# Relative bias written as eight rows and copied in DRAM for 128 queries, and RWKV's low-rank weights loaded and split in the indexer

## The chip, the cores and the metric

The kernel runs on one core of a Trainium2 chip. Times are device microseconds (us) of one execution. The kernel before took 1330.21 us, the median of 3 runs (1328.97 to 1335.14).

The engines are PE (TensorE: matrix products; PEld is its weight load), DVE (VectorE), ACT (ScalarE), POOL (GpSimd) and SP (SyncE, which issues nearly all DMAs of this kernel). Each engine takes its own instructions strictly in their order.

## What is computed

One inference step of a layer with three groups of heads, for 1024 new prompt rows and 64 new sample rows with 512 rows of history (1088 rows in all):

```
z = rms_norm(h, norm_g) @ w_in          # all branch columns from one projection
A: RWKV-7     zm = z + (prev - z) * mu;  r, k, v, w_in, a_in = split(zm)
              decay = exp(-exp(-softplus(-(w0 + tanh(w_in) @ w_b)) - 0.5))
              a     = sigmoid(a0 + a_in @ a_b)
              S = S * w + (S @ -kk) (kk * a)^T + v k^T;   y = S r   # a scan over the rows
B: forgetting attention
C: sparse attention: an indexer scores keys, the 256 best are kept,
              s = q . k * scale + t5_table[t5_bucket(pos_k - pos_q)]
h = h + concat(A, B, C gated) @ w_out;   y = rms_norm(h, final_g)
```

Two things matter here. `w_b` and `a_b` (64 x 512 each) are RWKV's low-rank weights. The relative bias of branch C depends on the distance of key and query alone: 8 heads by 384 distances hold all of it.

## The kernel before

The stages follow one another in one program: norm and transposes, the **indexer** (`indexer`), **RWKV** (17 units of four chunks, whose parts are braided), then the two attentions and the output. The projection `z` is made in column pieces of up to 128 (`proj`, L154: for each of 8 k-blocks three products, of `wb` with `uL` and of `wh` and `wl` with `uH`, for 384, 384 and 320 rows in turn). Its pieces are "fill": generators that `pump` calls between the steps of the main work. In the indexer the fill is the group `a0` of RWKV's columns and then `a1`.

A weight piece takes this way (`load_w`): SP issues the load of 512 KB into `wraw` (L130; two buffers), ACT casts it into `wh` (L137), POOL makes `wl` (L140, four instructions) and `wb` (L142, two). A product of the projection leaves PSUM from one of two banks, by ACT (`zs`, L802) and DVE (`zm`, L803, and `shift`, L805 and L806).

The order on each engine is not the order of the code alone. The framework's scheduler lays the instructions out by a simulated time line and by priorities, and takes what is ready in it; so a DMA that the code issues late can stand early in SP's queue.

**The bias.** `relative_bias` is a generator. Its first step loads the table and a one-hot matrix (L1250, L1251), its second makes the 8 x 384 product on PE (L1254) and copies it to `t5v` in SBUF, 8 partitions of 384 numbers (L1256). The third issues one DMA (L1258) that writes these eight rows 128 times into `d_t5` in DRAM, once for each of 128 queries. In the code the steps stand at i = 3, 5 and "s" of the indexer's loop over query blocks. `d_t5` is read again by the sparse attention (L1155). The profile calls it `d_t`.

**The low-rank weights.** `rwkv_pools`, behind the indexer, allocates `wabh` and `wabl`, clears `wabl` on POOL (L1271), loads each weight twice, for both halves of the partitions, into `wabr`, a buffer of the ring `z` (L1275, four DMAs of 128 KB), casts it on ACT (`wabh`, L1276) and makes the differences on POOL (`wabl`, L1278, two instructions). Each RWKV unit then begins with the products `low_rank` (L1293 with `wabh`, L1294 with `wabl`), with `wt` (L853), which is read back from DRAM, as the other operand, and with sums over squares (L1331).

Of the kernel before, what the change touches and what calls it, by code (L numbers as in the profile page):

```python
# [12 lines left out]
F32 = mybir.dt.float32  # L13
F32R = mybir.dt.float32r
# [4 lines left out]
OP = mybir.AluOpType  # L19
# [5 lines left out]
P = 128  # L25
# [60 lines left out]
class K:  # L86
# [311 lines left out]
    def indexer(self):  # L398
# [6 lines left out]
        with ExitStack() as c2:  # L405
# [54 lines left out]
            for i in list(range(2, 8)) + ["s"]:  # L460

                if i == 3:
                    gates = self.forget(ip, mrow)
                    next(gates)
                    bias = self.relative_bias(c2)
                    next(bias)
                if i == 4:
                    nc.sync.dma_start(out=O["p_c_kidx"][0, 0].rearrange("(a p) d -> p a d", p=P), in_=mrow[:, 0:8, 0:64])
                    nc.sync.dma_start(out=O["s_c_kidx"][0, 0], in_=mrow[:64, 8, 0:64])
                if i == 5:  # L470
                    next(bias)
                if i == 7:
                    next(gates, None)
                if i == "s":
                    next(bias, None)
                r = P if i != "s" else 64
                q0 = i * P - 256 if i != "s" else 768
                k0, kn = (0, (i + 1) * P) if i != "s" else (1024, 576)
                wi = 8 if i == "s" else i
                for s0 in range(0, kn, 512):  # L480
                    n = min(512, kn - s0)
                    for h in range(4):
                        ps = pm.tile([P, 512], F32, tag="s", name="ps_idx")
                        nc.tensor.matmul(ps[:r, :n], QI[h][:, q0:q0 + r], KI[:, k0 + s0:k0 + s0 + n], start=True, stop=False)
                        nc.tensor.matmul(ps[:r, :n], QI[h][:, q0:q0 + r], KIL[:, k0 + s0:k0 + s0 + n], start=False, stop=True)
                        rl = ip2.tile([P, 512], F32, tag="rl", name="rl")
                        nc.scalar.activation(rl[:r, :n], ps[:r, :n], AF.Relu, scale=0.125)
                        dst = self.score[i][:r, s0:s0 + n]
                        if h == 0:
                            nc.vector.tensor_scalar(dst, rl[:r, :n], wI[:r, wi, 0:1], None, op0=OP.mult)  # L490
                        else:
                            nc.vector.scalar_tensor_tensor(dst, rl[:r, :n], wI[:r, wi, h:h + 1], dst, op0=OP.mult, op1=OP.add)
                        if h % 2:
                            yield
                if i != "s":
                    nc.vector.memset(self.score[i][0:64, kn - 64:kn], NEG)
# [745 lines left out]
    def relative_bias(self, ctx):  # L1242

        nc = self.nc
        self.d_t5 = self.dram.tile([P, 8, 384], F32, tag="d_t5", name="d_t5")
        p = self.pool("t5", ctx=ctx, right=True)
        pp = self.pool("t5p", space=PSUM, ctx=ctx, right=True)
# [7 lines left out]
        vv = p.tile([8, 384], F32, name="t5v")  # L1255
        nc.vector.tensor_copy(vv, ps[:8, :384])  # L1256
        yield
        nc.sync.dma_start(out=self.d_t5.rearrange("q h r -> h q r"), in_=vv.rearrange("h (o r) -> h o r", o=1).broadcast_to([8, P, 384]))  # L1258


    def rwkv_pools(self, c2):


        nc, I, O = self.nc, self.I, self.O
        one = self.pool("rw1", ctx=c2, right=True)
        self.gen = self.pool("gen", space=PSUM, ctx=c2)
        self.gring = lambda tag, bufs: (lambda dt=F32: self.gen.tile([P, 512], dt, tag=tag, name="ps_" + tag, bufs=bufs))

        self.wabh = one.tile([P, 2, 512], F32R, name="wabh")
        self.wabl = one.tile([P, 2, 512], F32R, name="wabl")  # L1270
        nc.gpsimd.memset(self.wabl.bitcast(F32), 0.0)  # L1271
        raw = self.z("wabr")[:, 0:1024].rearrange("p (x c) -> p x c", x=2)
        for x, nm in enumerate(("a_w_b", "a_a_b")):
            for r in (slice(0, 64), slice(64, 128)):
                nc.sync.dma_start(out=raw[r, x], in_=I[nm][0])  # L1275
        nc.scalar.copy(self.wabh, raw)  # L1276
        for x, r in enumerate((slice(0, 64), slice(64, 128))):
            nc.gpsimd.tensor_tensor(self.wabl[r, x], raw[r, x], self.wabh[r, x], op=OP.subtract)  # L1278
        self.one, self.state = one, None

        self.ND = [one.tile([P, 2, 4, P], F16, name=f"ND{i}") for i in range(2)]
        for t in self.ND:
            nc.gpsimd.memset(t, 0.0)
# [472 lines left out]
def program(ctx, tc, I, O):  # L1756
# [24 lines left out]
    s.setup()  # L1781
    cx.close()
    with ExitStack() as c2:
        s.zs = s.pool("zs", bufs=1, ctx=c2, right=True)
        s.scp = s.pool("scp", ctx=c2, right=True)
        s.tkp = s.pool("tkp", ctx=c2, right=True)
# [19 lines left out]
        for u in range(n + 2):  # L1806
# [12 lines left out]
            if u < n:  # L1819
                work.append(("topk", topk, N_TOPK, (DVE, ACT)))  # L1820
            work = [w[:3] for w in work if w[0] != "topk"]
            s.free = u >= FE
            s.braid(work, R_T if u > n else R_END if len(work) < 3 and u else R_A / 10, ("topk", topk, N_TOPK, (DVE, ACT), work[-1][0] if SIDE < 0 else work[SIDE][0]) if u < n else None)
        for _ in topk:
# [89 lines left out]
```

## Time and profile before

| what | number |
|---|---|
| median of 3 runs | 1330.21 us |
| the profiled execution's own time | 1331.56 us |
| its span, first to last instruction | 1329.8 us |
| PE busy | 1258.4 us, 95% of the span |
| DVE, ACT, POOL busy | 847.5, 780.2, 669.7 us |
| mean granted clock of PE | 0.979 of full speed |
| DMA moved | 168.78 MB, mean 127 GB/s |

The numbers of the trace are from one profiled execution, whose span lies 1.8 us below its own time. "Busy" of PE is the time in which a product is under way, also at a lower clock. "Idle before" an instruction, in brackets in the time line, is the time in which its engine had nothing to do, with the work that ended the wait.

### The profile page before, as it was taken

The numbers are of one execution on the slowest core, as the hardware profiler recorded it, in microseconds if no ns is written. First come the engines' busy times: TensorE is split into PE (matmuls) and PEld (weight loads), VectorE is DVE, ScalarE is ACT, GpSimd is POOL, SyncE is SP. The second block draws the span as 40 slices with busy tenths as digits, with TensorE's granted clock in tenths as the row PEclk, the third lists the DMA queues.
The fourth block names the chain that finished last, engine by engine and source line by source line (L and its number), as shares of the span: only waits on it lengthen the run. The fifth ranks groups of instructions, "written<-read, shape, count | busy, mean of one in ns | idle before, by whom it ended". The sixth has DMA issues, their size and how long they took to land.

```text
span 1329.8 us, 29357 instructions
## 1 busy us (share of the span) xinstructions
PE 1258.4 (95%) x10544; PEld 964.2 (73%) x10563; DVE 847.5 (64%) x2487; ACT 780.2 (59%) x1762; POOL 669.7 (50%) x973
## 2 busy tenths in 40 slices
PE   7969999999999999988999998999999989999997
PEld 5747676777777777766777677888988856777764
DVE  7338437887877777899754316556666479766642
ACT  7335427777777887644353346576665578655532
POOL 6223445445445456556464365566667567544311
PEclk9979999999999999988999998999999989999999
DMA  7352422222223324433232378867755576543323
GB/s 224 50 105 71 128 83 66 87 70 89 68 70 104 102 80 140 123 101 110 94 104 89 126 216 246 217 201 209 182 198 146 146 212 186 142 116 106 97 76 95
DMA packets 172460, 168.78 MB, mean 127 GB/s; under 512 B 38513, under 2 KB 147097, under 8 KB 172314
## 3 DMA queue, kind: packets, MB, share of 16 engines
q1 hardware_dynamic: 172314, 166.89, 43.9%
q8 instruction: 84, 1.38, 0.4%
q14 instruction: 62, 0.51, 0.1%
HBM read 104.61 MB, written 62.24 MB: 125 GB/s over the span
## 4 chain that ended last, share of the span: by engine, by line
PE 73%; DVE 11%; DMA 6%; ACT 3%; issue 3%; POOL 2%; SPq 1%; DVEq 0%; POOLq 0%; ACTq 0%
PE pproj L154 32%; PE pproj L1697 7%; PE ps_pv L993 5%; PE ps_atp L107 5%; PE ps_tp L1697 4%; PE ps_ga L1412 3%; DMA wraw<-in_w_in_dram 2%; PE ps_sc L962 2%; PE ps_sc L963 2%; PE ps_gb L1471 2%; PE ps_tp L107 1%; PE ps_gb L1478 1%; PE ps_gc L1581 1%; ACT junka L601 1%; PE ps_gc L1583 1%
## 5 line engine op out<-in xcount | busy, mean ns | idle before, releaser
L154 PE MATMUL pproj<-uH,wh 128*128 128x384 f32 (+4 forms) x1088 | 494.6, 455 | 0.0
L154 PE MATMUL pproj<-uH,wl 128*128 128x384 f32 (+4 forms) x1088 | 363.4, 334 | 0.0
L154 PE MATMUL pproj<-uL,wb 128*128 128x384 bf16 (+4 forms) x1088 | 359.4, 330 | 2.2 <-DVE shift L806 2.0
L154 PEld LDWEIGHTS pproj<-uH,wh 128*128 128x128 f32 (+1 forms) x1088 | 217.9, 200 | 3.9 <-issue 0.7
L154 PEld LDWEIGHTS pproj<-uH,wl 128*128 128x128 f32 (+1 forms) x1088 | 208.1, 191 | 2.2 <-issue 0.2
L154 PEld LDWEIGHTS <-wb 128*128 128x128 bf16 (+1 forms) x1088 | 106.6, 98 | 118.6 <-issue 81.5
L601 ACT ACTIVATE junka<-score,tk_tau 128x1024 f16<-128x1024 f32 (+4 forms) x160 | 149.4, 934 | 38.9 <-DVE junk L595 24.1
L914 POOL TENSOR_SCALAR S<-S,mx 128x128 f32<-128x128 f32 (+8 forms) x136 | 103.8, 766 | 83.7 <-DVE mx L913 60.4
L931 ACT CAST hl<-ps_atp 128x512 fp32r<-128x512 f32 (+3 forms) x184 | 93.4, 514 | 77.7 <-PE ps_atp L107 68.2
L140 POOL TENSOR_TENSOR wl<-wraw,wh 128x256 fp32r<-128x256 f32 (+1 forms) x184 | 137.1, 775 | 3.3 <-ACT wh L137 2.7
L932 DVE TENSOR_TENSOR hl<-ps_atp,hl 128x512 fp32r<-128x512 f32 (+3 forms) x184 | 109.7, 600 | 44.6 <-ACT hl L931 42.8
L142 POOL TENSOR_SCALAR wb<-wraw 128x512 bf16<-128x512 f32 (+1 forms) x92 | 60.3, 671 | 142.1 <-issue 60.7
L909 ACT ACTIVATE S<-S,mx 128x128 f32<-128x128 f32 (+8 forms) x136 | 105.8, 778 | 38.2 <-DVE mx L905 34.8
L993 PE MATMUL ps_pv<-hl,VS 128*128 128x256 f32 (+3 forms) x640 | 113.7, 290 | 7.7 <-ACT hl L931 3.2
L993 PEld LDWEIGHTS ps_pv<-hl,VS 128*128 128x128 f32 (+1 forms) x640 | 90.4, 176 | 20.8 <-DVE hl L932 5.0
L107 PE MATMUL ps_atp<-ident,S 128*128 128x128 f32 x616 | 103.6, 280 | 1.1 <-POOL S L914 0.8
L1159 POOL TENSOR_TENSOR cb<-nm,T 128x256 f32<-128x256 bf16 (+2 forms) x80 | 57.4, 724 | 52.7 <-DVE mx L905 51.1
L107 PEld LDWEIGHTS ps_atp<-ident,S 128*128 128x128 f32 x616 | 76.4, 144 | 7.7 <-issue 1.7
L137 ACT CAST wh<-wraw 128x1024 fp32r<-128x1024 f32 (+1 forms) x46 | 47.7, 1038 | 47.0 <-PE pproj L154 27.0
L1697 PE MATMUL pproj<-oh,gh 128*128 128x512 f32 x144 | 67.4, 490 | 0.6 <-ACT pproj L1745 0.3
L803 DVE SCALAR_TENSOR_TENSOR zm<-pproj,omm,zs 128x384 f32<-128x384 f32 (+2 forms) x52 | 25.8, 496 | 43.3 <-ACT zs L802 42.9
L1697 PE MATMUL pproj<-ol,gb 128*128 128x512 bf16 (+1 forms) x134 | 48.8, 386 | 1.4 <-DVE ol L1677 0.9
(383 smaller groups left out, 2849.6 us busy)
## 6 DMA issues: line engine op xcount, KB each, us to landing
wraw<-in_w_in_dram SPq DMA_DIRECT2D x45, 512.0 KB
oraw<-in_w_out_dram SPq DMA_DIRECT2D x12, 512.0 KB
out_dram<-rows SPq DMA_DIRECT2D x10, 512.0 KB
x<-in_x_prompt_dram SPq DMA_DIRECT2D x8, 512.0 KB
wt<-a_wa SPq DMA_DIRECT2D x16, 256.0 KB
b_v<-vs SPq DMA_DIRECT2D x8, 512.0 KB
VS<-b_v SPq DMA_DIRECT2D x8, 512.0 KB
d_y<-y SPq DMA_DIRECT2D x64, 64.0 KB
```

Of the source, the lines that this page charges most:

```text
L107: self.nc.tensor.transpose(out, x, self.ident[:n, :n])
L140: nc.gpsimd.tensor_tensor(l[:, k:k + 2, :n], raw[:, k:k + 2, :n], h[:, k:k + 2, :n], op=OP.subtract)
L142: nc.gpsimd.tensor_scalar(b[:, k:k + 4, :n], raw[:, k:k + 4, :n], 1.0, 0.0, op0=OP.mult, op1=OP.add)
L154: self.nc.tensor.matmul(ps[:n, :nt], a[:, k, :n], b[:, k, t0:t0 + nt], start=(k == 0 and i == 0), stop=(k == KD - 1 and i == 2))
L601: nc.scalar.activation(junk[:, :sc.shape[1]], sc, AF.Sign, bias=tf[:, j:j + 1], accum_out=cnt[:, j:j + 1])
L909: nc.scalar.activation(S[:, :kn], S[:, :kn], AF.Exp, bias=mx[:, nm - 1:nm], scale=-1.0, accum_out=mx[:, 6:7])
L914: nc.gpsimd.tensor_scalar(S[:, :kn], S[:, :kn], mx[:, 7:8], 0.5, op0=OP.mult, op1=OP.mult)
L931: nc.scalar.copy(ph[:kr, a:b], ps[:kr, a:b])
L932: nc.vector.tensor_tensor(pl[:kr, a:b], ps[:kr, a:b], ph[:kr, a:b], op=OP.subtract)
L993: nc.tensor.matmul(pv[0:m, q0:256], VS[:, kb, 0:m], hl[:, x, o:o + w], start=kb == 0 and x == 0, stop=at[-1][0] == last and n == 3)
L1159: nc.gpsimd.tensor_tensor(o, x, y, op=OP.add)
L1697: nc.tensor.matmul(ps[hf][:n, :], parts[m // 4][q][:, m % 4, :n], self.wo[m][q // 2][:, hf * 512:hf * 512 + 512], start=m == 0 and q == 0, ...
```

## The change

It has two parts.

**The bias** is written as eight rows only: `t5v` goes to a new DRAM tile `d_row` (8 x 384), and eight DMAs copy `d_row` from DRAM to DRAM, each into 16 of the 128 queries of `d_t5`. In the code the row is written at i = "s" of the indexer's loop, and the copies are issued one by one at the beginning of RWKV's units 1 to 8.

**The low-rank weights** are loaded at i = 3 and split at i = 5 of the indexer's loop, into a pool of their own (`lr`). The raw weights lie in the tile of the scores of block 7, which is filled later.

```diff
                 if i == 3:
...
-                    bias = self.relative_bias(c2)
-                    next(bias)
+                    self.bias = self.relative_bias(c2)
+                    next(self.bias)
+                    self.load_low_rank()
...
                 if i == 5:
-                    next(bias)
+                    next(self.bias)
+                    self.split_low_rank()
...
                 if i == "s":
-                    next(bias, None)
+                    next(self.bias)
...
     def relative_bias(self, ctx):
+        row = self.dram.tile([8, 384], F32, tag="d_row", name="d_row")
...
         yield
-        nc.sync.dma_start(out=self.d_t5.rearrange("q h r -> h q r"), in_=vv.rearrange("h (o r) -> h o r", o=1).broadcast_to([8, P, 384]))
+        nc.sync.dma_start(out=row[:, :], in_=vv)
+        yield
+        for q in range(0, P, 16):
+            nc.sync.dma_start(out=self.d_t5[q:q + 16], in_=row.rearrange("(o h) r -> o h r", o=1).broadcast_to([16, 8, 384]))
+            yield
+    def load_low_rank(self):
+        nc, p = self.nc, self.lr
+        self.wabh = p.tile([P, 2, 512], F32R, name="wabh")
+        self.wabl = p.tile([P, 2, 512], F32R, name="wabl")
+        nc.gpsimd.memset(self.wabl.bitcast(F32), 0.0)
+        self.wabr = self.score[7].rearrange("p (x c) -> p x c", x=2)
+        for x, nm in enumerate(("a_w_b", "a_a_b")):
+            for r in (slice(0, 64), slice(64, 128)):
+                nc.sync.dma_start(out=self.wabr[r, x], in_=self.I[nm][0])
+    def split_low_rank(self):
+        nc.scalar.copy(self.wabh, self.wabr)
+        for x, r in enumerate((slice(0, 64), slice(64, 128))):
+            nc.gpsimd.tensor_tensor(self.wabl[r, x], self.wabr[r, x], self.wabh[r, x], op=OP.subtract)
...
     def rwkv_pools(self, c2):
-        self.wabh = one.tile([P, 2, 512], F32R, name="wabh")
-        self.wabl = one.tile([P, 2, 512], F32R, name="wabl")
-        nc.gpsimd.memset(self.wabl.bitcast(F32), 0.0)
-        raw = self.z("wabr")[:, 0:1024].rearrange("p (x c) -> p x c", x=2)
...
-                nc.sync.dma_start(out=raw[r, x], in_=I[nm][0])
-        nc.scalar.copy(self.wabh, raw)
...
             work = [w[:3] for w in work if w[0] != "topk"]
+            if u:
+                next(s.bias, None)
```

What stands on the engines is another matter than the code. SP's queue in the indexer, from the loads of the fourth and fifth weight piece on; `t5tab` and `t5oh` are the bias's operands, `score_416` is the tile of block 7's scores. Before:

```order
L130 DMA wraw<-in_w_in_dram 128x8x128 x2
L1250 DMA t5tab<-in_t_table_dram 32x8
L1251 DMA t5oh<-in_onehot_dram 32x384
L1258 DMA d_t_822<-t5v 8x128x384
L130 DMA wraw<-in_w_in_dram 128x8x128 x2
L468 DMA out_dram<-mrow 128x8x64
```

Now:

```order
L130 DMA wraw<-in_w_in_dram 128x8x128 x2
L1253 DMA t5tab<-in_t_table_dram 32x8
L1254 DMA t5oh<-in_onehot_dram 32x384
L1277 DMA score_416<-in_a_w_b_dram 64x512 x2
L1277 DMA score_416<-in_a_a_b_dram 64x512 x2
L1261 DMA d_row<-t5v 8x384
L1264 DMA d_t_826<-d_row 16x3072 x8
L130 DMA wraw<-in_w_in_dram 128x8x128 x2
L469 DMA out_dram<-mrow 128x8x64
```

The four weight loads, the row and all eight copies stand where the one DMA stood: ahead of the loads of the sixth and seventh weight piece, none of them between RWKV's units. The first copy waits for `d_row` to have landed.

PE's queue at the beginning of RWKV, around the first unit's low-rank products, among steps of the projection (one step is the three products of a k-block). Before:

```order
L154 MATMUL pproj<-uH,wh 128x320
L154 MATMUL pproj<-uH,wl 128x320
L1293 MATMUL ps_ga<-wt,wabh 128x256
L1294 MATMUL ps_ga<-wt,wabl 128x256
L1331 MATMUL ps_ga<-ones,k_1709 128x2 x2
L154 LDWEIGHTS wb
L154 MATMUL pproj<-uL,wb 128x320
```

Now:

```order
L154 MATMUL pproj<-uH,wh 128x384
L154 MATMUL pproj<-uH,wl 128x384
L1306 MATMUL ps_ga<-wt,wabh 128x256
L1307 MATMUL ps_ga<-wt,wabl 128x256
L154 LDWEIGHTS wb
L154 MATMUL pproj<-uL,wb 128x320
```

The two products moved ahead by four steps of 320 columns, and the sums over squares (now L1344) stand two steps behind them. Up to there PE's order is unchanged. From there on it changes in places to the end, because the simulated time line did: laid beside each other without their line numbers, about one of PE's rows in twelve stands elsewhere. On ACT the cast of `wabh` now stands between the casts of `KI` and `mT` of the third block of keys, and on POOL the clearing of `wabl` and its two differences stand ahead of the `wb` of the fourth weight piece.

## Rows read from the trace of the kernel before

**Rows 1.** The page: busy time of the engines, and PE's busy tenths in 40 slices of the span.

```profile
PE 1258.4 (95%) x10544; PEld 964.2 (73%) x10563; DVE 847.5 (64%) x2487; ACT 780.2 (59%) x1762; POOL 669.7 (50%) x973
...
PE   7969999999999999988999998999999989999997
```

**Rows 2.** Busy time by stretch, in us: the stretch, its length, then PE, PEld, DVE, ACT and POOL, PE's granted clock, the DMA engines' busy share and the GB/s they moved.

```profile
80.00:90.00 10.00, 2.35 (x8) 1.53 (x9) 4.25 (x12) 4.21 (x9) 4.05 (x6) 0.50 0.42 99
90.00:100.00 10.00, 10.00 (x50) 7.45 (x50) 7.95 (x26) 5.17 (x10) 2.93 (x4) 0.86 0.59 155
...
160.00:170.00 10.00, 6.88 (x33) 5.19 (x31) 1.91 (x4) 3.07 (x6) 4.12 (x5) 0.73 0.63 157
170.00:180.00 10.00, 10.00 (x59) 7.18 (x58) 4.37 (x13) 2.79 (x5) 6.01 (x11) 0.93 0.56 161
```

**Rows 3.** The time line of PE in the indexer: start, duration, engine, line, operation, and in brackets the idle time before it and what ended it.

```profile
74.89 0.34 PE L154 MATMUL pproj<-uL,wb 128*128 128x384 bf16 x1
...
75.42 0.34 PE L154 MATMUL pproj<-uL,wb 128*128 128x384 bf16 x1
...
75.77 0.34 PE L154 MATMUL pproj<-uH,wl 128*128 128x384 f32 x1
85.65 0.34 PE L453 MATMUL ps_tp<-ident,mT 76*64 76x76 f32 x1 [9.54 <-ACT mrow L454]
87.98 0.50 PE L154 MATMUL pproj<-uL,wb 128*128 128x384 bf16 x1 [2.00 <-DVE shift L806]
...
88.93 0.54 PE L154 MATMUL pproj<-uL,wb 128*128 128x384 bf16 x1
...
89.91 0.54 PE L154 MATMUL pproj<-uL,wb 128*128 128x384 bf16 x1
```

**Rows 4.** The time line of ACT, in the indexer and at the beginning of RWKV; columns as in rows 3.

```profile
47.16 0.42 ACT L425 COPY mT<-pproj 76x320 f32<-76x320 f32 x1 [1.56 <-PE pproj L154]
...
68.76 0.21 ACT L454 COPY mrow<-ps_tp 128x76 f32<-128x76 f32 x1
84.06 1.04 ACT L137 CAST wh<-wraw 128x1024 fp32r<-128x1024 f32 x1 [15.09 <-DMA wraw<-in_w_in_dram]
85.01 0.47 ACT L802 ACTIVATE zs<-pproj,par 128x256 f32<-128x256 f32 x1
...
158.06 0.51 ACT L1327 ACTIVATE k<-zt,par 128x256 f32<-128x256 f32 x1 [1.22 <-DMA zt<-a_k]
```

**Rows 5.** The chain of work that ended last in the first 240 us, in order of time: start, duration, and what ran (a DMA from its issue to its landing).

```profile
57.80 26.16 DMA wraw<-in_w_in_dram
...
154.02 0.39 SPq L853
...
158.80 4.26 DMA wabr<-in_a_a_b_dram
163.22 1.05 ACT wabh L1276
164.40 1.26 POOL wabl L1278
...
203.60 4.20 DMA wraw<-in_w_in_dram
```

**Rows 6.** The time line of SP's queue, 35 to 130 us: the start of an issue and how long it held the queue (for x2, from the first's start to the second's end).

```profile
40.47 0.33 SPq L1251 DMA_DIRECT2D t5oh<-in_onehot_dram  x1
49.62 0.29 SPq L1258 DMA_DIRECT2D d_t<-t5v  x1
57.80 17.71 SPq L130 DMA_DIRECT2D wraw<-in_w_in_dram  x2
```

**Rows 7.** DMA from 45 to 100 us, in 40 slices of 1.375 us: the busy share of the 16 DMA engines in tenths, the GB/s that they moved; and the size of the bias's transfer.

```profile
DMA  0000444444478444454444695445507077494940
GB/s 0 12 0 4 53 49 50 49 51 49 50 111 178 51 48 51 49 62 50 49 51 47 66 188 88 50 80 173 162 13 179 12 155 227 100 228 136 193 165 0
...
d_t<-t5v SPq DMA_DIRECT2D x1, 1536.0 KB
```

**Rows 8.** The time line of PE at the beginning of RWKV; columns as in rows 3.

```profile
164.32 0.38 PE L1293 MATMUL ps_ga<-wt,wabh 128*128 128x256 f32 x1 [2.12 <-ACT wabh L1276]
165.71 0.58 PE L1294 MATMUL ps_ga<-wt,wabl 128*128 128x256 f32 x1 [1.01 <-POOL wabl L1278]
```

**Rows 9.** The time line of POOL, in the indexer and at the beginning of RWKV; columns as in rows 3.

```profile
53.64 1.20 POOL L142 TENSOR_SCALAR wb<-wraw 128x512 bf16<-128x512 f32 x2 [21.27 <-PE pproj L154]
...
155.56 0.95 POOL L1271 MEMSET wabl<- 128x1024 f32 x1
...
164.40 2.60 POOL L1278 TENSOR_TENSOR wabl<-wabr,wabh 64x512 fp32r<-64x512 f32 x2 [6.05 <-ACT wabh L1276]
```

**Rows 10.** The instructions on the tile `fg`, its load: one row of 4 KB in DRAM read into each of 128 partitions (duration of the issue in ns, and its start in us).

```profile
L1654 SPq DMA_DIRECT2D fg<-in_final_g_dram x1: 536/536/536, 1065.1 to 1065.1; - x1
```

**Rows 11.** Busy time by stretch, columns as in rows 2: the indexer from 90 us on, RWKV with its fill, and the two us in which the load of `fg` ran.

```profile
90.00:150.00 60.00, 60.00 (x343) 44.92 (x342) 48.62 (x109) 32.84 (x65) 19.36 (x22) 0.98 0.29 83
...
180.00:750.00 570.00, 547.44 (x6258) 411.92 (x6256) 417.09 (x1282) 364.61 (x849) 294.75 (x449) 0.99 0.31 95
...
1066.00:1067.00 1.00, 0.15 (x1) 0.00 (x0) 1.00 (x1) 1.00 (x4) 0.12 (x1) 1.00 0.67 240
1067.00:1068.00 1.00, 0.00 (x0) 0.00 (x0) 1.00 (x6) 0.98 (x4) 0.00 (x0) 1.00 0.81 273
```

More of the change, by code (lines that the diff above doesn't have):

```diff
@@ L1257, in relative_bias @@
         yield
-        nc.sync.dma_start(out=self.d_t5.rearrange("q h r -> h q r"), in_=vv.rearrange("h (o r) -> h o r", o=1).broadcast_to([8, P, 384]))
+        nc.sync.dma_start(out=row[:, :], in_=vv)
[13 more added lines that the diff above has]
+    def split_low_rank(self):
+        nc = self.nc
+        nc.scalar.copy(self.wabh, self.wabr)
+        for x, r in enumerate((slice(0, 64), slice(64, 128))):
+            nc.gpsimd.tensor_tensor(self.wabl[r, x], self.wabr[r, x], self.wabh[r, x], op=OP.subtract)
     def rwkv_pools(self, c2):
@@ L1267, in rwkv_pools @@
         self.gring = lambda tag, bufs: (lambda dt=F32: self.gen.tile([P, 512], dt, tag=tag, name="ps_" + tag, bufs=bufs))
-        self.wabh = one.tile([P, 2, 512], F32R, name="wabh")
-        self.wabl = one.tile([P, 2, 512], F32R, name="wabl")
-        nc.gpsimd.memset(self.wabl.bitcast(F32), 0.0)
-        raw = self.z("wabr")[:, 0:1024].rearrange("p (x c) -> p x c", x=2)
-        for x, nm in enumerate(("a_w_b", "a_a_b")):
-            for r in (slice(0, 64), slice(64, 128)):
-                nc.sync.dma_start(out=raw[r, x], in_=I[nm][0])
-        nc.scalar.copy(self.wabh, raw)
-        for x, r in enumerate((slice(0, 64), slice(64, 128))):
-            nc.gpsimd.tensor_tensor(self.wabl[r, x], raw[r, x], self.wabh[r, x], op=OP.subtract)
         self.one, self.state = one, None
@@ L1783, in program @@
     with ExitStack() as c2:
+        s.lr = s.pool("lr", ctx=c2, right=True)
         s.zs = s.pool("zs", bufs=1, ctx=c2, right=True)
```

## The prediction, made before the changed kernel ran

> **What bounds the kernel now.** I read the page first: PE is busy for 95% of the span, and of its 40 slices the third is the only low one behind the first [rows 1]. So a microsecond is gained where PE is idle or runs at a low clock, and the change touches two such places. Busy time by stretch shows both: 2.35 us of PE work at half clock from 80 to 90 us, and 6.88 us at a mean of 0.73 from 160 to 170 us [rows 2].
>
> The first place is a gap in the indexer. PE ends a product at 75.77 + 0.34 = 76.1 us, is idle 9.54 us, does one transpose, is idle 2.00 us more, and goes on at 87.98 us [rows 3]. It waits for a PSUM bank, which ACT and DVE have to empty. ACT was ready at 69.0 us, but its next instruction is the cast of a weight piece, which waits 15.09 us for `wraw`; the `zs` that empties the bank stands behind it and runs at 85.01 us [rows 4]. That load was issued at 57.80 us and took 26.16 us, where another of the same size took 4.20 us [rows 5]. SP shows why it was late: the bias's DMA went out at 49.62 us, ahead of it, and the two weight loads behind took 17.71 us to go out [rows 6]. From 50.5 us to about 82 us the DMA engines are at 0.4 of their time and near 50 GB/s; 1,536 KB (1.573 MB) at 50 GB/s is 31.5 us, which is that stretch [rows 7].
>
> The second place is the beginning of RWKV: PE waits 2.12 us for `wabh` and 1.01 us for `wabl` [rows 8]. The chain there runs from the landing of the raw weights through the cast to the difference [rows 5].
>
> **Part 1, the gap.** It removes 9.54 + 2.00 = 11.5 us of idle PE. After it PE ran at half clock: the clock of 0.86 from 90 to 100 us makes a slow stretch of 10 x 0.14 / 0.5 = 2.8 us, to 92.8 us [rows 2]. A step of the projection takes 89.91 - 88.93 = 0.98 us there and 75.42 - 74.89 = 0.53 us before the gap, a factor of 1.85 [rows 3]. The 4.8 us from 87.98 us would be 2.6 us without the idle time ahead of them: 2.2 us. Together 13.7 us, if the weight lands in time.
>
> When is that? From its landing at 84.06 us to PE's next product 3.9 us went by [rows 3, 4]. The bank is wanted at 76.1 us, so a landing up to 72.2 us costs nothing.
>
> What stands ahead of it now is the row and eight copies, one behind another as in the new order of SP, and not between RWKV's units. The row goes out at about 49.6 us as the old DMA did; no row shows so small a write, and I take the 4.2 us of a whole weight load [rows 5] as its upper bound: the copies begin by 54.1 us (estimate). Their eight issues at some 0.3 to 0.6 us are through before 57.8 us, when the weight's buffer comes free anyway. No copy from DRAM to DRAM is in the trace, so I bound its rate. Slow end: 50 GB/s, the rate of the transfer that they replace [rows 7]; they end at 54.1 + 31.5 = 85.6 us, the weight lands 4.2 us later, at 89.8 us. Middle: that transfer kept 0.44 x 16 = 7 engines busy; sixteen at the same rate each give 114 GB/s, 13.8 us, and the weight lands at 72.1 us, just in time. Fast end: the load of `fg`, too, reads one DRAM row many times [rows 10], and while it ran the DMA moved 240 to 273 GB/s [rows 11]; a copy that reads and writes at half of that takes 11.5 us, and the weight lands at 69.8 us; at the whole rate, 64 us. I take the half rate, because `fg` is the nearest row, and so no idle time is left.
>
> Here a rule bears on the choice. The Trainium skill, "DMA: Bandwidth & Descriptors", section "Why a DMA increments its semaphore by 16 and not by 1", says that a DMA runs on as many engines, at most 16, as divide the slowest dimension of both its sides. By it the old DMA, with 8 rows outermost, had 8 engines, and a copy, with 16 outermost, has all; the 7 busy engines agree. By the rule the sum stays as below; by the old transfer's row alone, 50 GB/s whatever the shape, it would be the first rival.
>
> What is late next, with the gap gone? From 90 to 150 us PE is busy all 60 us, with DVE at 48.6 us in the same order [rows 11], so PE sets that stretch; the slow clock gave DVE 2.2 us to get ahead, and that much could come back as a wait. I take 0 and keep 2.2 us for the range.
>
> **Part 2, the low-rank weights.** It removes 2.12 + 1.01 = 3.1 us of idle time. The slow clock lasts to 170 + 10 x 0.07 / 0.5 = 171.4 us; from 165.71 us [rows 8] that is 5.7 us, which at 1.85 would be 3.1 us: 2.6 us. Together 5.7 us. What it adds lies elsewhere. The four loads go out behind `t5oh`, at 40.8 us, and the DMA is nearly idle from 45 to 50 us [rows 6, 7]; with four issues of up to 0.6 us and the 4.26 us that the last took to land [rows 5] they are there near 47 us. The cast of 1.05 us comes where ACT is idle 1.56 us [rows 4], and the wait for the loads may hold ACT 2 us longer. I take 0 for that, since PE is busy there with products that are under way, and keep 2 us for the range. On POOL the clearing (0.95 us) and the differences (2.60 us) fall into a wait of 21.27 us [rows 9]. Without that cover they would cost POOL 3.6 us, which the weights' own lead hides. Next late would be `wt`: it went out at 154.02 us [rows 5], ahead of the `zt` that ACT's square had got by 158.06 us [rows 4], and PE takes the products four steps earlier than 164.32 - 2.12 = 162.2 us, so at about 160.1 us. No wait is left.
>
> **The sum.** 13.7 + 5.7 = 19.4 us. All engines go through one order, and no stage is tied to a fixed time, so what PE gains at 88 and at 166 us moves all that follows. The profiled execution's own time is 1331.56 us: 1312.2 us. The median is 1.35 us lower, 1330.21 us: **1310.8 us**, 1.5% faster.
>
> The unknown is the new order. From 180 to 750 us PE is idle 570 - 547.4 = 22.6 us [rows 11], in hundreds of short waits on RWKV's chains, and one row in twelve stands elsewhere there. It can give some of that back or add to it; I take 0, with 8 us to either side.
>
> **The rivals.**
> - *The copies run at the old rate.* Against it: more engines, rows of 12 KB in one piece in place of 1.5 KB, and `fg`'s rate. For it: no row shows such a copy. The weight lands at 89.8 us, 5.7 us later than before, which eats the 5.7 us of part 2: 1330.2 us, no change.
> - *Slower: the copies hold the weights up longer than the old DMA did.* Place: the sixth weight piece, behind the copies in SP's queue. A copy reads and writes DRAM on the same engines; at half of 50 GB/s it takes 62.9 us, the weight lands at 121.2 us, 37.1 us later, and the sum is 37.1 - 5.7 = +31.4 us: 1361.6 us. It decides from 50 GB/s down, and below 41 GB/s the kernel is slower by over 0.5%.
> - *The new order costs what the gaps gave.* If PE's idle time in RWKV grew by half, 11.3 us, the time would be 1322.1 us. For it: PE's waits there depend on what stands beside what. Against: the same scheduler made both orders.
> - *The new order gives more:* a third of that idle time gone, 7.5 us, makes 1303.3 us.
>
> **How the numbers follow.** The forecast, with the order within 8 us to either side, gets 0.73; the order costing more than 8 us 0.09, half of it beyond 0.5%; the order giving more than 8 us 0.06; the old rate 0.07; slower copies 0.05. A measurement of this kernel tells about 0.5%, 6.7 us, from no change, so the line is at 1323.6 us. Faster: 0.73 + 0.06 + 0.045, rounded 0.84. Within: 0.045 + 0.07, 0.11. Slower: 0.05. The range runs from 1301 to 1323 us: it takes in the 2.2 us of DVE, the 2 us of ACT and nearly all orders, and leaves out both rivals of the copies and the worst orders, about 2 in 10.
>
> **What the profile will show.** If part 1 is right: the sixth weight lands before 72 us, PE has no wait for `mrow` or `shift` near 76 us, and its clock stays at full speed to 150 us; the copies take 6 to 14 us. If part 2 is right: no wait of PE for `wabh` or `wabl`, and full clock over the beginning of RWKV, now near 146 us. If the order is neutral: PE idle 15 to 30 us over RWKV. The prediction is wrong if the weight lands after 72 us, or if PE's idle time in RWKV grows by more than 12 us.

## The result, and the profile after

The changed kernel takes 1316.77 us, the median of 6 runs (1315.02 to 1323.17), beside 1332.68 us (1328.24 to 1337.24) of the kernel before in the same session: a ratio of 0.9897, 95% interval 0.9877 to 0.9917. By the ratio that is 13.7 us less (11.1 to 16.4), by the medians 15.9 us, where 19.4 us were forecast (a ratio of 0.985); the ratios compare fast runs alone, the medians take all. The time is 6.0 us above the forecast of 1310.8 us; 2.5 us of these are the kernel before, whose median was 1330.21 us in the runs shown then. The profiled execution took 1316.68 us, 14.9 us less than the one of before.

The page, lines as in [rows 1]: PE has as much work as before in a shorter span, and the third slice is full.

```profile
PE 1261.2 (96%) x10563; PEld 965.1 (73%) x10563; DVE 846.3 (64%) x2487; ACT 781.1 (59%) x1762; POOL 672.1 (51%) x973
...
PE   7999999999999999989999998999999988999997
```

Busy time by stretch, columns as in [rows 2]; then all of RWKV with its fill, as in [rows 11], and ten us in it:

```profile
80.00:90.00 10.00, 10.00 (x61) 7.68 (x59) 9.76 (x22) 5.38 (x9) 6.30 (x8) 1.00 0.43 109
90.00:100.00 10.00, 9.53 (x58) 7.25 (x56) 7.51 (x25) 5.23 (x12) 0.96 (x2) 1.00 0.44 114
90.00:150.00 60.00, 59.53 (x358) 44.60 (x356) 41.35 (x89) 29.91 (x63) 20.24 (x25) 1.00 0.35 102
160.00:170.00 10.00, 10.00 (x66) 7.38 (x64) 2.66 (x9) 3.69 (x8) 5.65 (x9) 1.00 0.22 71
...
160.00:735.00 575.00, 554.34 (x6266) 416.37 (x6264) 415.94 (x1282) 365.68 (x849) 294.19 (x449) 0.98 0.31 95
...
460.00:470.00 10.00, 8.41 (x78) 6.08 (x74) 7.23 (x19) 6.13 (x14) 5.61 (x10) 0.83 0.59 200
```

Both places that were to gain are full, or nearly so, and at full clock; RWKV's beginning, now near 146 us, lies in the third row. What is new is in the last two rows: RWKV has no more idle time than before (575 - 554.34 = 20.7 us, 22.6 us before), but its clock is 0.98 where it was 0.99, and there are stretches like that from 460 us on.

SP's queue, as in [rows 6], and DMA from 45 to 100 us, as in [rows 7]:

```profile
49.07 0.28 SPq L1261 DMA_DIRECT2D d_row<-t5v  x1
50.48 4.95 SPq L1264 DMA_DIRECT2D d_t<-d_row  x8
57.22 5.46 SPq L130 DMA_DIRECT2D wraw<-in_w_in_dram  x2
```

```profile
DMA  0000069992910580000007094691950000198900
GB/s 12 0 0 9 0 286 286 295 277 34 292 56 0 123 258 0 0 12 0 6 8 182 9 266 118 139 256 29 187 199 0 0 0 0 76 316 255 178 5 0
```

The first copy goes out 1.4 us behind the row, the eight move 277 to 295 GB/s, and the transfers are through near 57 us, where the old DMA kept its 50 GB/s until 82 us. The weight loads behind need 5.46 us in place of 17.71 us to go out.

ACT and PE where the gap was, and PE at RWKV's beginning, columns as in [rows 3]:

```profile
71.31 1.05 ACT L137 CAST wh<-wraw 128x1024 fp32r<-128x1024 f32 x1 [2.89 <-PE pproj L154]
```

```profile
75.39 0.23 PE L453 MATMUL ps_tp<-ident,mT 76*64 76x76 f32 x1
75.46 0.33 PE L154 MATMUL pproj<-uL,wb 128*128 128x384 bf16 x1
...
146.18 0.28 PE L1306 MATMUL ps_ga<-wt,wabh 128*128 128x256 f32 x1
146.29 0.28 PE L1307 MATMUL ps_ga<-wt,wabl 128*128 128x256 f32 x1
```

The cast no longer waits for a DMA [rows 4], and none of these PE instructions has a bracket, so none waited [rows 3, 8].

### The profile page after: what moved, and what is told of

Read it like the earlier page. It is cut to its first block, busy times and chain, and to the rows that moved or that the text cites. A ratio compares the mean times of both kernels' runs of the same rounds, so it can differ in the third digit from the quotient of the medians.

```text
span 1314.9 us, 29369 instructions
## 1 busy us (share of the span) xinstructions
PE 1261.2 (96%) x10563; PEld 965.1 (73%) x10563; DVE 846.3 (64%) x2487; ACT 781.1 (59%) x1762; POOL 672.1 (51%) x973
## 4 chain that ended last, share of the span: by engine, by line
PE 56%; DVE 7%; DMA 3%; ACT 3%; issue 1%; POOL 1%; SPq 0%; DVEq 0%; POOLq 0%; ACTq 0%
PE pproj L154 21%; PE pproj L1710 7%; PE ps_pv L995 5%; PE ps_atp L107 4%; PE ps_tp L1710 4%; PE ps_sc L964 2%; PE ps_sc L965 2%; PE ps_ga L1425 2%; PE ps_tp L107 1%; PE ps_gb L1484 1%; PE ps_gb L1491 1%; PE ps_gc L1594 1%; PE ps_gc L1585 1%; ACT junka L603 1%; PE ps_gc L1596 1%
## 5 line engine op out<-in xcount | busy, mean ns | idle before, releaser
L995 PEld LDWEIGHTS ps_pv<-hl,VS 128*128 128x128 f32 (+1 forms) x640 | 90.6, 176 | 20.1 <-DVE hl L934 4.6
L1710 PE MATMUL pproj<-ol,gb 128*128 128x512 bf16 (+1 forms) x144 | 52.4, 386 | 0.9 <-DVE ol L1690 0.9
L1710 PE MATMUL pproj<-oh,gl 128*128 128x512 f32 x120 | 46.7, 399 | 0.0
```

Of the source, the lines that this page charges most:

```text
L995: nc.tensor.matmul(pv[0:m, q0:256], VS[:, kb, 0:m], hl[:, x, o:o + w], start=kb == 0 and x == 0, stop=at[-1][0] == last and n == 3)
L1710: nc.tensor.matmul(ps[hf][:n, :], parts[m // 4][q][:, m % 4, :n], self.wo[m][q // 2][:, hf * 512:hf * 512 + 512], start=m == 0 and q == 0, ...
```

## Where the gain is and where it goes again

To follow a gain through a program, I took every PE instruction that both kernels have, and its start in the trace of before minus its start in the other trace. The table gives the median of this lead, in us, for the instructions that started in the 20 us that begin at the time in the head, in the trace of before; the last column is the end. Kernels are named below.

| kernel | 100 | 200 | 280 | 300 | 480 | 740 | 1000 | end |
|---|---|---|---|---|---|---|---|---|
| after | 14.1 | 20.1 | 22.1 | 20.0 | 16.9 | 16.1 | 16.8 | 14.9 |
| after again (e3) | 13.5 | 19.4 | 21.4 | 19.3 | 16.2 | 19.0 | 19.7 | 17.6 |
| row in DRAM, old shape (e4) | 14.1 | 20.0 | 22.1 | 18.5 | 15.4 | 19.8 | 19.3 | 16.7 |
| other form (e5) | 13.7 | 19.7 | 21.7 | 17.0 | 13.5 | 15.7 | 16.8 | 13.6 |
| one copy (e8) | 12.3 | 18.3 | 20.3 | 18.2 | 15.0 | 17.2 | 18.4 | 14.8 |
| low-rank weights alone (e2) | 0.5 | 6.4 | 8.4 | 2.6 | -1.0 | -1.2 | -1.0 | -4.0 |
| bias alone (e1) | 13.4 | 13.7 | 13.7 | 13.7 | 14.1 | 13.9 | 14.4 | 9.6 |
| two pieces without `wl` (e6) | 13.3 | 19.2 | 21.3 | 21.6 | 21.4 | 20.0 | 21.6 | 20.2 |
| `wb` of two on ACT (e7) | 13.8 | 19.8 | 21.8 | 22.0 | 22.0 | 23.2 | 22.4 | 17.0 |
| `wl` of two on DVE (e10) | 12.8 | 18.7 | 20.7 | 20.9 | 18.9 | 14.4 | 15.2 | 13.7 |
| both off POOL (e11) | 14.4 | 20.3 | 22.4 | 22.4 | 21.4 | 22.9 | 22.7 | 18.3 |

The row of after: the gap gives 14 us, RWKV's beginning 6 us more. Another 2 us come between 200 and 280 us, in every kernel with part 2 and not in e1; no term of the forecast has them. Between 280 and 480 us 5 us go again. Two places hold most of that. The first, near 280 us; DVE, POOL and PE, columns as in [rows 3]:

```profile
279.13 3.60 DVE L617 TENSOR_TENSOR tk_tau<-tk_tau,tk_t 128x8 int32<-128x8 int32 x1
```

```profile
278.76 1.20 POOL L142 TENSOR_SCALAR wb<-wraw 128x512 bf16<-128x512 f32 x2
279.93 2.78 POOL L140 TENSOR_TENSOR wl<-wraw,wh 128x256 fp32r<-128x256 f32 x4
```

```profile
283.66 0.67 PE L1434 MATMUL ps_ga<-rk,ones 128*128 128x256 f32 x2 [2.48 <-DVE BA L1429]
```

A DVE instruction on 8 columns, of the top-k search of the indexer's scores, takes 3.60 us; its median is 0.167 us. It begins while POOL works on a weight piece, and ends at 282.73 us, when the last of POOL's six instructions ends (282.71 us). What stands behind it on DVE is late, and PE waits 2.48 us. Such a hold isn't wholly new. The trace of before has a shorter one at another place, beside three POOL instructions without a gap between them, and PE waits 0.72 us behind it:

```profile
553.54 1.78 DVE L615 TENSOR_TENSOR tk_tau<-tk_tau,tk_t 128x8 int32<-128x8 int32 x1
```

```profile
553.45 0.39 POOL L1417 TENSOR_SCALAR ND<-BN 64x256 f16<-64x256 f32 x1
553.82 1.48 POOL L699 TENSOR_TENSOR kl<-kT,kh 128x272 fp32r<-128x272 f32 x2
```

The second place, near 462 us, DVE, POOL and PE:

```profile
460.41 0.94 DVE L1383 TENSOR_TENSOR BK<-BK,Pi 128x256 f32<-128x256 f32 x1
461.28 0.94 DVE L1386 TENSOR_TENSOR QR<-QR,Pt 128x256 f32<-128x256 f32 x1
462.15 0.71 DVE L617 TENSOR_TENSOR tk_tau<-tk_tau,tk_t 128x8 int32<-128x8 int32 x1
```

```profile
458.75 3.19 POOL L140 TENSOR_TENSOR wl<-wraw,wh 128x256 fp32r<-128x256 f32 x4
461.91 1.65 POOL L701 TENSOR_TENSOR zq<-zq,qh 128x272 f32<-128x272 f32 x2
```

```profile
463.25 0.37 PE L1491 MATMUL ps_gb<-T,ND 128*128 128x64 f16 x4 [1.12 <-DVE T L1527]
```

Again DVE is stretched, here beside POOL's `wl` and `zq`, PE waits 1.12 us, and behind it PE's clock is at its lower level for 3.4 us (the row of 460 to 470 us above, at 0.83). The two waits stand in all six traces of this order (after, e2 to e5, e8), with 2.46 to 2.48 us and 1.11 to 1.12 us; in before and e1 PE has no wait of over 1 us between 250 and 500 us. My theory from here on: **the new order puts DVE instructions of a short chain beside POOL's weight pieces, and what the two gaps gave is partly lost there.** The rival: the new order is a little worse in many places, and these two only show it.

## The experiments

### Each part alone, the change again, and the old shape (e1 to e4)

e1 is the kernel before with the row and the eight copies; e2 is the changed kernel with the old DMA of the bias; e3 is the changed kernel once more. In e4 only the copies change:

```diff
-        for q in range(0, P, 16):
-            nc.sync.dma_start(out=self.d_t5[q:q + 16], in_=row.rearrange("(o h) r -> o h r", o=1).broadcast_to([16, 8, 384]))
-            yield
+        nc.sync.dma_start(out=self.d_t5.rearrange("q h r -> h q r"), in_=row.rearrange("h (o r) -> h o r", o=1).broadcast_to([8, P, 384]))
```

> Part 1 alone: the row and the eight copies, with the low-rank weights loaded and split at RWKV's beginning as before. Its order on PE, DVE, ACT and POOL is word for word the order of the kernel before; only SP's queue differs. My theory (the old DMA made the gap near 80 us, and it is the new order, which part 2 alone brings, that takes time back in RWKV): the gap is gone, everything from 100 us on stands about 13.5 us earlier, the low clock between 450 and 650 us lasts about 14 us as before, and the time is 13 to 15 us under the kernel before, the same as the changed kernel within 2 us. Rival (the time taken back in RWKV is chance of the execution): the same 13.5 us, but the low clock in RWKV is any number from 7 to 24 us. Rival (part 1 itself disturbs RWKV): less than 10 us are gained.

> Part 2 alone: the low-rank weights loaded and split in the indexer, with the one old DMA for the bias. Its order on PE and DVE is word for word that of the changed kernel. My theory: the gap near 80 us stays, the waits for wabh and wabl are gone (6 us earlier behind 170 us), and the new order takes about 5 us of it back between 450 and 650 us by a low clock of some 24 us there: 0 to 3 us under the kernel before. Rival (chance of the execution, order neutral): 5 to 7 us under the kernel before, low clock in RWKV about 14 us.

> The changed kernel once more, nothing edited: how far its time and the low clock in RWKV repeat. My theory (the order sets them): the low clock between 450 and 650 us again lasts 20 to 27 us, in the same places (near 463, 576 and 606 us), time 12 to 16 us under the kernel before. Rival (chance): the low clock there is another length or place, such as 10 to 15 us near 580 us alone.

> The changed kernel with one DMA in place of the eight copies, from the row in DRAM, but in the old shape: 8 rows outermost, 128 queries, 384 numbers each (packets of 1,536 bytes). All other orders unchanged. Theory A (the shape made the old DMA slow: few engines, short packets at a stride of 12 KB): DMA share near 0.4 to 0.5 and about 50 GB/s for 31 us from 51 us on, the weight lands near 86 us, the gap is back, and the time is 13 to 16 us over the changed kernel. Theory B (the source made it slow, one SBUF partition for each engine): half the engines at some 20 GB/s each, the transfer ends in 8 to 10 us, no gap, the time of the changed kernel within 2 us.

| kernel | median (runs) | ratio to before, 95% interval |
|---|---|---|
| before, in the same session | 1331.58 us (17) | |
| e1 | 1322.18 us (6) | 0.9917, 0.9895 to 0.9939 |
| e2 | 1332.36 us (12) | 1.0001, 0.9976 to 1.0025 |
| e3 | 1315.57 us (5) | 0.9875, 0.9851 to 0.9899 |
| e4 | 1316.41 us (4) | 0.9877, 0.9840 to 0.9915 |

**The parts don't add up.** By the ratios the bias alone gives 11.1 us, the low-rank weights alone nothing, both together 16.6 us (e3). The difference is hardly beyond the intervals; the table of leads shows it place by place. Laid beside each other without line numbers, e1 has the order of before on PE and DVE, and e2, e3 and e4 have the order of after: so the new order comes from part 2 alone. The table shows what that means. e1 keeps its 13.7 us through all of RWKV. e2 leads by 8.4 us at 280 us; 5.8 us of that go by 300 us, and by 480 us all of it. The 3.59 us instruction is in e2, e3 and e4 too. In e2, PE's clock drops behind the wait; busy time by stretch:

```profile
295.00:305.00 10.00, 7.70 (x52) 5.72 (x52) 7.09 (x22) 4.94 (x11) 3.42 (x6) 0.58 0.36 111
```

The same wait of about 2.5 us was followed by no low clock in after, e3 and e8, by 3.4 us of it in e4, 6.8 us in e5 (below) and 10.2 us in e2. So behind one and the same wait the lead falls by 2 to 6 us, by one trace of each kernel.

**Not all of after's loss is the order's.** Two expectations failed. e1 was to gain 13 to 15 us and to equal the changed kernel; it gains 11.1 us and is 6.6 us slower than e3. e3, the changed kernel once more, was to have 20 to 27 us of low clock between 450 and 650 us again. It has 13.6 us, as many as before, where after has 23.8 us; a spell of 10.2 us near 606 us is missing. e3's lead at 740 us is 19.0 us, after's 16.1 us. This difference lies between two executions of one kernel.

**Where the old DMA lost its time** is told by e4: DMA from 45 to 100 us, as in [rows 7].

```profile
DMA  0000045555890580000007094690950000199900
GB/s 0 12 0 9 0 168 194 199 202 202 266 280 14 117 264 0 0 12 0 0 9 187 4 247 142 136 253 16 203 203 0 0 0 0 66 322 255 173 7 0
```

With the old shape, 8 rows outermost, half of the DMA engines are busy, as in the old DMA (0.44), but they move 194 to 202 GB/s in place of 50. What differs is the source: eight rows in DRAM in place of eight partitions of SBUF, read 128 times each. The shape gives the rest, from 200 to some 290 GB/s, and that is worth nothing here, since 200 GB/s is soon enough. On the number of engines, the rule that the prediction cited (the Trainium skill, "DMA: Bandwidth & Descriptors", section "Why a DMA increments its semaphore by 16 and not by 1") agrees with the 0.5 of e4. The factor of 4 between the two sources is not one of engines, since about half of them are busy with either.

### One copy in place of eight (e8)

```diff
-        for q in range(0, P, 16):
-            nc.sync.dma_start(out=self.d_t5[q:q + 16], in_=row.rearrange("(o h) r -> o h r", o=1).broadcast_to([16, 8, 384]))
-            yield
+        nc.sync.dma_start(out=self.d_t5[:, :, :], in_=row.rearrange("(o h) r -> o h r", o=1).broadcast_to([P, 8, 384]))
```

> The changed kernel with one copy for all 128 queries in place of eight for 16 queries each; the order on PE and VectorE stays as it was. If only the source in DRAM counts, the copy still takes 5 to 8 us, the weight piece behind it lands before 72 us and the time stays at 1314 to 1319 us. If the parts count (one transfer of 1.57 MB runs at fewer or slower queues), the copy takes over 12 us, TensorE waits near 76 us again, and the time rises towards 1330 us.

1317.62 us (4 runs), 0.9870 (0.9852 to 0.9888) of 1334.99 us. The parts don't count: that the copies are spread over RWKV's units is in the code only, the scheduler issues all of them in the indexer, and one DMA does the same.

### The held instruction in another form (e5)

```diff
-                v.tensor_tensor(tau, tau, t1, op=OP.bitwise_xor)
+                v.scalar_tensor_tensor(tau, tau, 0, t1, op0=OP.bitwise_or, op1=OP.bitwise_xor)
```

> The changed kernel with the top-k step's update of its threshold (tk_tau xor tk_t, 31 of them) written as scalar_tensor_tensor in place of tensor_tensor; the order of instructions on PE and DVE stays as it was. In three traces with the new order the one near 279 us takes 3.6 us in place of 0.15 us and ends when POOL's six weight instructions (3.95 us in a row) end, and TensorE then waits 2.5 us. Theory A: VectorE is held up by POOL because this instruction reads two tiles of SBUF, in whatever form: it still takes over 2.5 us there, and the time stays within 1315 to 1318 us. Theory B: it is the form alone that is held up: the instruction falls under 0.4 us, the 2.5 us wait goes, and the time falls to about 1314 us.

1317.99 us (6 runs), 0.9872 (0.9853 to 0.9891) of 1334.99 us. The group in its trace (ns: least, median, most):

```profile
L617 DVE SCALAR_TENSOR_TENSOR tk_tau<-tk_tau,tk_t x31: 151/168/3587, 200.6 to 543.9; 128x8 int32<-128x8 int32 x31
```

It is held as long as before: the form is not the reason, and theory B of this run falls.

### POOL relieved at the two places (e6, e7, e10, e11)

The two weight pieces that POOL works on near 280 and 459 us are the 17th and the 24th. e6 leaves their `wl` out; e10 makes it on DVE; e7 makes their `wb` on ACT; e11 does as e10 and e7.

```diff
+        e = nc.vector if len(self.loaded) in (16, 23) else nc.gpsimd      # e10, e11
         for k in range(0, KD, 2):
-            nc.gpsimd.tensor_tensor(l[:, k:k + 2, :n], raw[:, k:k + 2, :n], h[:, k:k + 2, :n], op=OP.subtract)
+            e.tensor_tensor(l[:, k:k + 2, :n], raw[:, k:k + 2, :n], h[:, k:k + 2, :n], op=OP.subtract)
+        if len(self.loaded) in (16, 23):                                  # e7, e11
+            nc.scalar.copy(b[:, :, :n], raw[:, :, :n])
...
```

> The changed kernel with POOL's four subtractions (wl) left out for two of the 46 weight pieces, those that POOL works on near 280 and 459 us; the projections of these two read wh in the place of wl. The order in RWKV changes somewhat with it. Theory A (the loss of the new order is VectorE held up by POOL at these two places): POOL's train near 280 us is 1.2 us in place of 3.95, the held instruction takes under 1.5 us, TensorE's waits near 284 us (2.5 us) and 463 us (1.1 us) go and the 3.4 us of half clock behind the second with them (1.7 us): 1311 to 1314 us. Theory B (the new order as a whole costs, these two places are only where it shows): the loss comes up elsewhere in RWKV, 1315 to 1318 us.

> The changed kernel with wb of the same two weight pieces cast on ACT in place of POOL (1.05 us each there); everything is still computed, and the order changes at these places and after. Theory A: POOL's train near 280 us falls from 3.95 to 2.8 us, so the wait of TensorE behind it falls by 1.2 us or goes with the changed order: 1313 to 1316 us. Theory B: no gain, 1315 to 1319 us, and the waits come up at other places.

> The changed kernel with the four subtractions (wl) of the two weight pieces near 280 and 459 us done by VectorE in place of POOL; everything is computed. The order changes with it. Theory A (POOL's trains at these two places hold VectorE up): the loss in RWKV goes as it did when they were left out, less about 2 us of VectorE's own work in each: 1310 to 1315 us. Theory B (any new order costs): 1315 to 1320 us.

> As the kernel before it, with wb of the two pieces cast on ACT too, so that POOL does nothing for them. Theory A: 1309 to 1314 us, no held instruction near 280 us and TensorE without a wait of over 1.5 us between 250 and 480 us. Theory B: 1315 to 1320 us.

| kernel | median (runs) | ratio to before, 95% interval |
|---|---|---|
| before, beside e5 to e8 | 1334.99 us (11) | |
| e6 | 1310.70 us (4) | 0.9815, 0.9797 to 0.9833 |
| e7 | 1314.57 us (5) | 0.9848, 0.9828 to 0.9868 |
| before, beside e10 and e11 | 1332.22 us (11) | |
| e10 | 1316.94 us (6) | 0.9888, 0.9861 to 0.9914 |
| e11 | 1318.00 us (6) | 0.9899, 0.9866 to 0.9931 |

Each of the four changes the order as well: counted in the traces, 4% (e7, e11) to 12% (e10) of PE's instructions and 6 to 17% of DVE's stand elsewhere than in after. In all four the hold of 3.6 us is gone (that instruction takes at most 0.84 us in their traces), and the table of leads shows no loss from 280 to 300 us; three of them (e6, e7, e11) still have over 21 us at 480 us, where after has 16.9. So far the theory holds: without the hold at the first place, the forecast's 19.4 us go through RWKV in these three.

At the second place the lead holds in e6 and e10. In e7, where `wl` stays on POOL, and in e11, where POOL has neither piece, PE still waits near 460 us:

```profile
459.53 0.28 PE L1494 MATMUL ps_gb<-T,ND 128*128 128x64 f16 x4 [1.11 <-DVE T L1530]
```

That is e7's; in e11 it is 1.23 us. But PE's clock stays at its upper level behind it, and the lead falls there by 1.6 us in both, where it falls by 3.2 us in after. So about half of the second loss is the clock's, and with both pieces off POOL the other half is still there.

The time at the end follows in e6 alone. e7 and e11 lose 4 to 5 us behind 1000 us, in the attention; e10 has a wait of PE of 2.4 us for DVE elsewhere in RWKV, lies at 14.4 us by 740 us, and is no faster than after. e6 also leaves 5.6 us of POOL's work out (eight `wl` instructions at 0.7 us). It is 7 us faster than e5 and e8, which have the order of after and ran beside it; by its ratio it gains 24.6 us, more than the two gaps' 19.4 us, so more than the lost time is in it. So e6 shows no more than that the two places are worth at most some 7 us, and e10 and e11 that moving the work elsewhere doesn't get it back. Their times are those of the rival theory (1315 to 1320 us), though e11 has no wait of PE of over 1.5 us between 250 and 480 us, as the theory expected.

e7 is the fastest kernel that computes everything, but its interval, clear of after's, overlaps with those of e3, e5 and e8: that it beats the changed kernel isn't settled.

### The held instruction by itself (e9, e12)

Both are the changed kernel with a tail behind its last result, in which POOL runs trains like that of a weight piece and DVE runs a few instructions beside each; so their total times say nothing. The core of e9's:

```diff
+    for op in ops:                     # six forms of a DVE instruction on f (SBUF), f1 (SBUF), ps (PSUM)
+        g.memset(f[:, c8], 1.0)        # POOL; the train and the DVE instructions read f
+        for k in range(0, KD, 4):
+            g.tensor_scalar(b[:, k:k + 4], raw[:, k:k + 4], f[:, 0:1], 0.0, op0=OP.mult, op1=OP.add)
+        for k in range(0, KD, 2):
+            g.tensor_tensor(l[:, k:k + 2], raw[:, k:k + 2], f.rearrange("p (k c) -> p k c", k=2), op=OP.subtract)
+        for i in range(3):
+            op()
```

> The changed kernel with a tail behind its last result: six times POOL runs a train like that of a weight piece (two tensor_scalar of 128x512, four tensor_tensor of 128x256, about 4 us) which begins with a memset of a tile that three equal VectorE instructions then read, so that these start inside the train. The six instructions, in order: tensor_tensor 128x8 with two tiles of SBUF, tensor_scalar 128x8 with one, tensor_tensor 128x256 with two, tensor_scalar 128x256 with one, tensor_tensor 128x256 with one tile of SBUF and one of PSUM, scalar_tensor_tensor 128x256 with two of SBUF. Theory A (the number of SBUF tiles read decides): the first, third and sixth take over twice their time alone (0.15 and 0.4 us) or up to the whole train, the fifth takes about 0.4 us. Theory B (any instruction beside POOL's train can be held): the fifth is stretched as much. Theory C (VectorE is not held up by POOL, the 3.6 us have another reason): all near 0.15 and 0.3 to 0.5 us.

The six groups of its trace, three instructions each (ns: least, median, most; the least is the first, which began just ahead of POOL's first):

```profile
L1930 DVE TENSOR_TENSOR pr_zf<-pr_f,pr_f x3: 168/567/632, 1319.6 to 1320.4; 128x8 f32<-128x8 f32 x3
```
```profile
L1931 DVE TENSOR_SCALAR pr_zf<-pr_f x3: 172/578/632, 1324.0 to 1324.8; 128x8 f32<-128x8 f32 x3
```
```profile
L1932 DVE TENSOR_TENSOR pr_zf<-pr_f,pr_f x3: 424/795/795, 1328.3 to 1329.6; 128x256 f32<-128x256 f32 x3
```
```profile
L1933 DVE TENSOR_SCALAR pr_zf<-pr_f x3: 295/664/668, 1333.2 to 1334.2; 128x256 f32<-128x256 f32 x3
```
```profile
L1934 DVE TENSOR_TENSOR pr_zf<-pr_f,pr_ps x3: 421/422/422, 1337.7 to 1338.6; 128x256 f32<-128x256 f32 x3
```
```profile
L1935 DVE SCALAR_TENSOR_TENSOR pr_zf<-pr_f,pr_f x3: 424/795/795, 1342.1 to 1343.3; 128x256 f32<-128x256 f32 x3
```

The DVE instruction that reads PSUM takes 0.42 us beside POOL, three times. Those with all operands in SBUF are held up: 0.17 us becomes 0.57 to 0.63 us, 0.30 us becomes 0.66 us, 0.42 us becomes 0.80 us. That holds for one tile read as for two, so theory A's condition, two tiles, falls; that POOL holds DVE up stands, and C falls. What is not there is a hold over a whole train. e12 lets an instruction of 128x8, on two tiles of SBUF, meet the train at nine moments.

> As the kernel with the tail of trains, with other contents of the tail: nine trains of POOL in the forms of a weight piece (two tensor_scalar of 128x512 with constants, four tensor_tensor of 128x256 with wh), and in each one VectorE instruction that reads PSUM, of 8 to 512 columns in steps of 64, and behind it one tensor_tensor of 128x8 with two tiles of SBUF. So the small instruction meets the train at nine moments, some 0.07 us apart. Theory A (where it meets POOL's running instruction decides how long it is held): in some trains it is held to the train's end, over 2 us, in others for one POOL instruction, up to 0.75 us. Theory B (one POOL instruction is the most that it is held for, and the 3.6 us near 280 us have something else behind them): never over 0.8 us.

Its group over the nine, and two of them, DVE behind the PSUM instruction that sets the moment:

```profile
L1937 DVE TENSOR_TENSOR pr_z<-pr_d,pr_big x9: 171/361/608, 1319.3 to 1353.3; 128x8 f32<-128x8 f32 x9
```

```profile
1340.53 0.17 DVE L1937 TENSOR_TENSOR pr_z<-pr_d,pr_big 128x8 f32<-128x8 f32 x1
1344.12 0.63 DVE L1936 TENSOR_SCALAR pr_d<-pr_ps,pr_big 128x392 f32<-128x392 f32 x1 [3.42 <-POOL pr_big L1931]
1344.78 0.61 DVE L1937 TENSOR_TENSOR pr_z<-pr_d,pr_big 128x8 f32<-128x8 f32 x1
```

In every train the small instruction ends within 0.1 us of the end of the POOL instruction that was running when it began: theory B of this run. So the rest of one POOL instruction is what a hold costs here. That fits the second place, near 462 us: three DVE instructions in a row take 0.94, 0.94 and 0.71 us, where instructions of their sizes take 0.42 and 0.17 us alone. But in both tails each DVE instruction that was held began beside one of the two `tensor_scalar` of a train; none began beside a `tensor_tensor`.

The 3.60 us near 280 us lasted over five POOL instructions more, in six traces of the same order, and neither tail repeats that. In the old order, too, holds went over several POOL instructions, at two other places: the 1.78 us shown above (also in e1) and, in before, this one, each over two more:

```profile
627.87 1.74 DVE L655 TENSOR_TENSOR tk_need<-tk_need,tk_cnt 64x1 f32<-64x1 f32 x1
```

That the instruction near 280 us is of int32 is no reason by itself: this one is of f32, and in e6, e7, e10 and e11 the same int32 instruction is held for 0.84 us at most.

## Why the prediction was right, and by what it was off

**Part 1, 13.7 us.** Right: the lead at 100 us is 12.3 to 14.4 us in the ten traces of the table that have the gap closed. The weight is cast at 71.31 us, and what that cast waited for was a product of PE. The step on the copies' rate was too low: I took half of `fg`'s rate, 11.5 us; they ran at the whole rate, near 290 GB/s, and took about 6 us. With the weight's buffer free at 57 us that changes nothing. The 2.2 us that DVE might give back came as a wait of 0.47 us (9.53 us busy from 90 to 100 us).

**Part 2, 5.7 us.** Right on the spot: 6 us of lead more between 100 and 200 us in every trace that has it, with nothing held on ACT or POOL by the earlier cast and the differences.

**The new order, taken as 0.** This is the term that was mis-sized. Of 20 us of lead at 200 us, 14.9 us are left at the end in the profiled execution, and 13.6 to 17.6 us in four more kernels of the same order. By the ratios of after, e3, e4, e5 and e8 (0.9870 to 0.9897 of 1330 us) the change gives 13.7 to 17.3 us, 2 to 6 us short of 19.4. The loss sits inside the 8 us that the range allowed, but it isn't all the noise that I took it for: 5 to 9 us go between 280 and 480 us in each of the six traces of this order, mostly at the two places above, and none in e1; 0 to 4 us come back up to 1000 us, and 2 to 4 us go behind it. How long the clock stays low is noise in part, as after and e3 show. And 2 us that the new order gave between 200 and 280 us, which I had not forecast, made up for some of the loss: luck. The order changed more than I wrote: counted in the traces, one PE instruction in eight stands elsewhere, and one in five on DVE, where the two places are.

**My test for it was blind.** "PE idle 15 to 30 us over RWKV" came true, 20.7 us, with the loss in it: the lower clock makes PE busy for longer and not idle. The row to ask for is the granted clock beside the idle time.

**The rivals.** The two on the copies fell by their rate. "The order costs" was right in kind, but at a fifth to a half of the 11.3 us that it was priced at.

**Open:** why one DVE instruction was held for 3.60 us; why e1, whose order is that of before, loses 4.8 us behind 1000 us (two waits of PE of 2.1 us for a load of `cQ` are part of it); why e7 and e11 lose 4 to 5 us there; how much of the loss in RWKV is the holds' and how much the clock's; and whether part 2 in the old order would give all of its 6 us, since no kernel here has that order.

## What to carry to other kernels

A gain that closes a gap is measured at the gap, but a scheduler that lays everything out by simulated time gives a new order behind it; price that order apart, with the lead of like instructions stage by stage, and expect a few us either way. A broadcast that is read many times from a few SBUF partitions can be written once to DRAM and copied there: 50 became 200 to 290 GB/s. Look for short DVE instructions that PE waits for beside POOL's long SBUF trains; one fed from PSUM was not held in e9. Whether keeping them apart gains time in a whole kernel is not shown: e10 and e11 gained nothing, and e7's 3 us aren't settled. An edit that gains nothing alone (e2) can still be worth some 3 to 6 us with its partner.

## What the runs showed of the hardware

- DVE instructions on SBUF alone wait for the POOL instruction that is running (0.17 to 0.57 or 0.63 us, 0.42 to 0.80 us), one with an operand in PSUM does not (0.42 us). In the kernels some waited for several in a row (3.60, 1.78 and 1.74 us); why is open. The Trainium skill, "GPSIMD Engine Reference", section "8. Key points", says that POOL shares its SBUF interfaces with VectorE and contends with instructions of two SBUF inputs or in a two-port mode. The runs agree on two inputs; that the one-input `tensor_scalar` was held as well fits only by the second condition, and no run here shows the mode.
- The same wait of PE of 2.5 us was followed by full clock in some executions, and by 3.4, 6.8 or 10.2 us at the lower level in others.
